# One pool group's u as a block product, in a hybrid attention and pooling layer

## The chip, the cores and the metric

The kernel runs on one core of one Trainium2 chip. The metric is the device time of one execution in microseconds. Several executions are timed, and the median counts; one more is recorded by the hardware profiler and gives the trace that is read below.

## The reference

One layer of a generator's backbone, for 1024 latent tokens and 256 context tokens of width 1024, in float32. A normalised and modulated input `h` goes through one wide projection, whose columns feed two branches. Branch A is a gated linear attention with four heads, run in both directions. Branch B is a pooling mixer in four groups of 256 columns, with windows of 2, 4, 8 and 16 tokens. Both are gated, projected, merged by sigmoid gates, projected again and normalised. What matters here is branch B and the projection that feeds it:

```python
p = h @ w_in
... uB, zB, gA, gB = jnp.split(p, idx, axis=-1)
# multiscale_pool: per group g with window w
parts.append((csg[:, hi + 1] - csg[:, lo]) / cnt - uf[..., sl])   # windowed mean minus u
y = einsum(d, w_pool) * pool_scale
yB = (y * jax.nn.silu(zB)) @ w_branch_b
```

## The kernel before

Matrices are kept transposed: `h^T` lies in eight row tiles of 128 rows, each in two token halves of 512 columns. To keep float32's precision every operand is split into a high and a low part (`split`, line 82: ScalarE writes the high part, VectorE the rest by a tensor_tensor of 512 columns), and a product is made of three matmuls, high x high, high x low and low x high. All matmuls are recorded on line 77.

There are two forms of a product. The plain one (`proj_t`, line 273) makes 128 output rows for 512 tokens by 8 x 3 matmuls into one PSUM bank, which ScalarE then empties. `pool_u` (line 643) and `pool_gate` (line 624) call it four times for a group, so 96 matmuls; their weights come by `wslot` (line 245), one load of 512 KB and two splits for 128 columns. The block form (`block_product`, line 797) makes 256 output rows for all 1024 tokens by seven products of blocks in place of eight (Winograd's form), each of 4 x 3 matmuls, so 84. The seven are, in order, L11 R11, S2 T2, S3 T3, S1 T1, L12 R21, L22 T4 and S4 R22. L and S are pieces of the weights: `block_weights` (line 762) loads two raw tiles, makes four sums or differences and splits all seven; this is called at high priority. R and T are operands of `h^T`: three of them are tiles of `h^T` itself, and T2, T3, T1, T4 are made once by `operands_h` (line 741) for each of four pairs of row tiles, with four additions, four subtractions and four splits on VectorE, in temporary tiles (tags `A` and `sw`, for the fourth pair `wh` and `wl`). The results are put in `h_ops` and serve all later block products. `take` (line 811) empties the banks: ScalarE copies product 1 into the output, VectorE adds the others. The banks are taken in the cycle sc, pj, sc, pj, pj (line 794), with two banks of tag sc and three of pj, so product 6 uses the bank of product 1.

Each pool group needs `u` (its columns of the projection), the gate `zb`, the difference `d` of the windowed mean and u (`pool_diff`, line 651: for each of two row tiles, passes over 1024 columns on VectorE, then a split of each token half) and the mix (`pool_mix`, line 688: 24 matmuls, a multiplication with the gate and the operands of the next product, which are written to DRAM). The groups are taken in the order 1, 0, 2, 3 (line 850). The tile of `u` has the tag `t8` with one slot: the next `u` can be written only when `d` has read the one before; GpSimd then fills the edges of the new tile (lines 639 and 640).

A framework orders the work. The program gives it the instructions with their tiles; when it is built, each engine's queue is laid out by priority (program order, with the weights of block products ahead) and by when operands and tile slots come free, and every wait is set by it. Tags with few slots matter here: `wr` (raw weights) 2, `wh` and `wl` (split weights) 4 each, `A` and `sw` 2 each, `t8` 1. Before the stretch around the change the last attention head uses most of them. The part that the change touches (lines 881 to 889):

```python
u[0] = pool_u(order[0])
zb[0] = pool_gate(order[0])
d[0] = [pool_diff(order[0], u[0][:, m, :]) for m in range(2)]
u[1] = pool_u(order[1])
for _ in range(4):
    add_h_ops()
pool_mix(order[0], d[0], zb[0])
d[1] = [pool_diff(order[1], u[1][:, m, :]) for m in range(2)]
u[2] = pool_u_blocks(order[2])
```

In the rows below the tile names are the tags: `t` is the tile of u, `z` a temporary of `pool_diff`, `qk` the gate, `s` the split difference, `ppj` and `psc` PSUM banks.

Of the kernel before, what the change touches and what calls it, by code (L numbers as in the profile page):

```python
# [34 lines left out]

# slots of the one SBUF pool, by tag; PSUM banks, by tag
BUFS = dict(h=32, wr=2, wh=4, wl=4, z=2, t8=1, lr=5, s2=8, sw=2, v=8, qk=8, bx=1, A=2, kt=2, S=6, S0=4, on=1,
# [5 lines left out]
def hybrid_kernel(ctx: ExitStack, tc: tile.TileContext, x, ctx_in, rows, w_mod, b_gate_row,  # L43
# [38 lines left out]
    def split(hi, lo, src):  # L82
        """src = hi + lo, exactly, both float32r"""
        act(hi, src)
        tt(lo, src, hi.bitcast(F32), ALU.subtract)
# [3 lines left out]

    # ---- constants and small vectors as columns  # L90
    cst = const("cst", [P, N_CONST])
    load(cst, consts)
    ident = cst[:, C_ID:C_ID + P]
    ones = cst[:, C_ONE:C_ONE + P]
# [15 lines left out]

    # ---- token tiles: load, root mean square, normalise
    pow_in = const("pow_in", [P, 10])
# [21 lines left out]

    # ---- low-rank gate inputs, stacked parts on partitions
    def low_rank_weights():
# [16 lines left out]

    # ---- modulation: shift and scale as columns [d, (latent, context)]
    sA = const("sA", [P, KT, 2])
# [7 lines left out]
    def modulate(kt, t0, n, c, ptag):  # L163
        """psum of one row tile of xn^T and the scale and shift that make it h^T"""
        pt = PT(ptag)
        for i in range(n // P):
            nc.tensor.transpose(pt[:, i * P:(i + 1) * P],
                                xs[t0 + i][kt // 4][:, (kt % 4) * P:(kt % 4 + 1) * P], ident)
        return pt[:, :n], sA[:, kt, c:c + 1], shA[:, kt, c:c + 1]
# [31 lines left out]
    for b in range(4):  # L201
        s_, half_ = b % 2, b // 2
        c0 = s_ * D + half_ * HALF
# [3 lines left out]
        for kt in range(KT):  # L207
# [8 lines left out]
            hi, lo = T("wh", [P, HALF], F32R), T("wl", [P, HALF], F32R)  # L216
# [24 lines left out]

    # ---- weight stream: slots of 1024 columns, split into exact float32r parts
    ahead = [False]

    def wslot(src, shape, col_scale=None):
        """rows [p, k, n] of a weight; per k: (hi, lo)"""
        _, nk, n = shape
        per = HALF // n
        parts = []
        with tc.high_priority() if ahead[0] else nullcontext():  # L250
            raw = T("wr", shape)
            load(raw, src)
            if col_scale is not None:
                tt(raw, raw, col_scale.rearrange("p (k n) -> p k n", k=1).to_broadcast(shape), ALU.mult)
            for k0 in range(0, nk, per):
                kn = min(per, nk - k0)
                hi, lo = T("wh", [P, kn, n], F32R), T("wl", [P, kn, n], F32R)
                split(hi, lo, raw[:, k0:k0 + kn, :])
                parts += [(hi[:, i, :], lo[:, i, :]) for i in range(kn)]
        return parts  # L260
# [4 lines left out]
    def wquad(w, c0, col_scale=None):  # L265
        """256 columns, all rows"""
        parts = []
        for kh in range(2):
            src = w[kh * HALF:(kh + 1) * HALF, c0:c0 + 256]
            parts += wslot(src.rearrange("(k p) n -> p k n", p=P), [P, 4, 256], col_scale)  # L270
        return parts

    def proj_t(w, rhs_hi, rhs_lo, n):
        """psum[128 columns, n tokens] = W^T h"""
        pt = PT("pj")
        nk = len(w)
        for k in range(nk):
            whi, wlo = w[k]
            mm(pt[:, :n], whi, rhs_hi[k], k == 0, False)
            mm(pt[:, :n], whi, rhs_lo[k], False, False)  # L280
            mm(pt[:, :n], wlo, rhs_hi[k], False, k == nk - 1)
        return pt

    def proj_n(w, lhs_hi, lhs_lo, tok):
        """psum[128 tokens, 256 columns] = h W"""
        pt = PT("pj")
        for k in range(KT):
            whi, wlo = w[k]
            mm(pt[:, :256], lhs_hi[k][:, tok], whi, k == 0, False)
            mm(pt[:, :256], lhs_hi[k][:, tok], wlo, False, False)  # L290
            mm(pt[:, :256], lhs_lo[k][:, tok], whi, False, k == KT - 1)
        return pt
# [25 lines left out]

    # ---- context: final states of both directions
    S0 = [None] * NH  # L320
# [28 lines left out]
    def transpose_k(src, tag):  # L349
        """four of [dk, 128] -> [token, chunk, dk]"""  # L350
        pt = PT("tr")
        for i in range(CPH):
            nc.tensor.transpose(pt[:, i * P:(i + 1) * P], src[i], ident)  # L353
        kT = T(tag, [P, CPH, P])
        act(kT, chunks(pt))
        return kT
# [32 lines left out]

    # ---- latent heads  # L390
    def rope_apply(pt, hf, scale):
# [37 lines left out]

    # Queries and keys lie with their two decays side by side: slot 1 is what a left block gives to the  # L430
    # scores with its right neighbour (backward decay of queries, forward of keys), slot 0 is for right blocks.
    # Decays of tokens and blocks: array 0 has the backward one of the even and the forward one of the odd,
    # array 1 the others.
    DEC_OFF = {2: 0, 4: 256, 8: 384, 16: 448, 32: 480, 64: 496, 128: 504}
# [8 lines left out]
    def level(t, hl):  # L443
        """slot 1 of the even blocks of hl tokens and slot 0 of the odd ones: [pair, block, token]"""
        t = t.rearrange("p n d -> p (n d)").rearrange("p (g x) -> p g x", x=4 * hl)[:, :, 1:4 * hl - 1]
        return t.rearrange("p g (s r) -> p g s r", s=2)[:, :, :, 0:2 * hl - 1:2]

    def gates(h):
        """per half: decays of the tokens, and of the blocks of 2, 4, .. 128 tokens"""
        both = T("bx", [P, 2, 2, HALF])  # L450
        e, one = [both[:, hf] for hf in range(2)], [None, None]
        for hf in (1, 0):
            one[hf] = [T("s2", [P, HALF]) for _ in range(2)]
            for d in range(2):
                pt = PT(('o', 'tr', 'sc', 'sc')[2 * hf + d])
                bcol = gate_in(pt, h, d, hf + 1, HALF)
                for t in range(2):
                    a = 0 if d != t else 1
# [30 lines left out]
    def double_q(hl, t, dec):  # L489
        """from blocks of hl tokens to blocks of 2 hl"""  # L490
        t = level(t, hl)
        dec = dec.rearrange("p (g s n) -> p g s n", s=2, n=1)[:, :, ::-1, :]
        tt(t, t, dec.to_broadcast([P, HALF // (2 * hl), 2, hl]), ALU.mult)

    def double_k(hl, cur, rest, dec):
        """the same; cur meets its sibling in the scores of a level"""
        shape = [P, HALF // (4 * hl), 2, hl]
# [6 lines left out]
    def head_scores(h, st, decays):  # L504
        """per half: scores within chunks; queries and keys with the decay up to the ends of their chunk:
        qf, qb, kf, kb by chunk; and the decays of the chunks, forward and backward"""
        one, e = decays
# [78 lines left out]

    # ---- context states and latent heads
    msk_f = T("bx", [P, len(LEVELS), P])
# [33 lines left out]

    # ---- pooling branch
    def pool_gate(g):
# [26 lines left out]
    def pool_diff(g, u):  # L651
        """split tiles of (windowed mean - u)^T for one row tile"""
        w = WINDOWS[g]
# [44 lines left out]

    # ---- products of 2 x 2 blocks by seven block products (Winograd's form):
    #      row blocks m of W^T, inner blocks j (odd and even row tiles), token halves hf  # L700
    half_tile = {}

    def slot2(tag, dt=F32R):
        """two tiles of 512 columns"""
        if tag in ("t8", "bx"):
# [17 lines left out]
    def block_operands(o, val):  # L723
        """splits the operands of a row tile pair from the values of R11, R12, R22, R21 (overwritten)"""
        def put(n, v):
# [15 lines left out]
    def operands_h(g, tags, temps):  # L741
        """block operands of h^T, row tiles 2g and 2g + 1"""
        k0, k1 = 2 * g, 2 * g + 1
# [53 lines left out]
    def block_product(w, c0, ops, outs, post, by_rows=False, pre=None):  # L797
        """outs[m][hf] = (W^T X) of two column tiles from c0; post(m, hf) when one is done"""
        with tc.high_priority():
# [46 lines left out]

    # ---- pool groups; block operands of h^T meanwhile
    h_tags = {"T2": ["v"] * 4, "T3": ["lr", "lr", "S0", "S0"], "T1": ["S", "S", "S", "A"], "T4": ["bx", "bx", "kt", "sw"]}
# [34 lines left out]
    zb[0] = pool_gate(order[0])  # L883
    d[0] = [pool_diff(order[0], u[0][:, m, :]) for m in range(2)]
    u[1] = pool_u(order[1])
    for _ in range(4):
        add_h_ops()
    pool_mix(order[0], d[0], zb[0])
    d[1] = [pool_diff(order[1], u[1][:, m, :]) for m in range(2)]
# [12 lines left out]

    # ---- gates of the merge
    def release_order(tags):
# [37 lines left out]
    for i in range(2):  # L942
        for mp in range(4):
            if (i, mp) != (0, 0):
                gate_pair(i, mp)
            if (i, mp) == (1, 1):
                gb_ops.append(gb_operands(0))
    # ---- pool branch output
    gb_ops += [gb_operands(g) for g in range(1, 4)]
# [16 lines left out]

    # ---- attention branch output, merged
    freed = release_order(b_tags)
# [34 lines left out]

    # ---- output projection, residual and final norm
    mH = [[None] * KT for _ in range(2)]
# [107 lines left out]
```

## Time and profile before

| | |
|---|---|
| median of three runs | 1150.31 us |
| lowest and highest run | 1150.07 and 1152.89 us |
| span of the profiled execution | 1152.8 us |
| TensorE (PE) busy | 1119.6 us, 97% |
| VectorE (DVE) busy | 812.2 us, 70% |
| ScalarE (ACT) busy | 493.4 us, 43% |
| mean granted clock of TensorE | 0.995 |

Of the profiled execution's own time only the span is known; it lies 0.1 us under the slowest of the three runs and 2.5 us over their median. The profile has a page with busy times, the span in 40 slices, queues, the chain of work that ended last and the costliest groups; and views of stretches of it, of which a timeline lists the instructions of an engine with their start, their length and, in brackets, how long the engine stood idle before and what released it. Matmuls overlap, so their listed lengths add up to more than the time they take; their pace is read from many in a row.

### The profile page before, as it was taken

The page shows a single profiled execution, that of the slowest core. Times are in us where ns is not written, and L with a number is a line of the kernel's source. Part 1 is how long each engine was busy: PE and PEld are TensorE (multiplying, and loading weights), DVE is VectorE, ACT ScalarE, POOL GpSimd, SP SyncE. Part 2 cuts the span into 40 slices and gives each one's busy share as a digit, 9 for nine tenths or more (in the row PEclk, how much of TensorE's full clock was granted, in tenths as well). Part 3 has the DMA queues.
Part 4 walks back from the last instruction along what each step waited for, and adds up shares of the span by engine and source line. Part 5 has one row for each costly group of instructions (what it writes and reads, how often), then busy time and mean ns, then how long its engine had stood idle before and what let it go on. Part 6 is the DMA issues. An engine that isn't in the chain of part 4 may idle for free.

```text
span 1152.8 us, 16292 instructions
## 1 busy us (share of the span) xinstructions
PE 1119.6 (97%) x5993; PEld 926.7 (80%) x5993; DVE 812.2 (70%) x1533; ACT 493.4 (43%) x962; POOL 24.2 (2%) x50
## 2 busy tenths in 40 slices
PE   6799999999999999999999999999999999999997
PEld 1268998798798798788888888888887886878997
DVE  4677458488588587698988867665768776757454
ACT  6697552462452552543333433343446324113233
POOL 0100000000000000100000000000000000000001
PEclk9899999999999999999999999999999999999999
DMA  8812150120220310103251463524448468982113
GB/s 292 291 37 74 42 151 28 56 73 20 65 65 20 85 44 20 55 28 119 82 161 50 128 201 119 167 84 129 151 137 269 161 197 287 298 302 94 38 38 146
DMA packets 119660, 138.40 MB, mean 120 GB/s; under 512 B 8803, under 2 KB 80669, under 8 KB 119454
## 3 DMA queue, kind: packets, MB, share of 16 engines
q1 hardware_dynamic: 119582, 137.38, 37.6%
q8 instruction: 47, 0.77, 0.3%
q14 instruction: 31, 0.25, 0.1%
HBM read 100.65 MB, written 32.51 MB: 116 GB/s over the span
## 4 chain that ended last, share of the span: by engine, by line
PE 86%; DMA 6%; ACT 2%; DVE 2%; issue 2%; SPq 1%; POOL 1%; POOLq 0%; ACTq 0%; DVEq 0%
PE ppj L77 59%; PE psc L77 19%; PE pst L77 3%; PE po L77 2%; DMA h<-w_mod 1%; DMA qk<-ga 1%; PE ptr L77 1%; DMA qk<-x 1%; DMA qk<-gb_T 1%; DMA wr<-w_in 1%; PE ptr L353 1%; ACT sw L63 1%; SPq L80 1%; DMA wr<-w_b 0%; DMA S<-ctx 0%
## 5 line engine op out<-in xcount | busy, mean ns | idle before, releaser
L77 PE MATMUL ppj<-h,wh 128*128 128x512 f32 x794 | 257.9, 401 | 1.0 <-ACT h L63 1.0
L63 ACT ACTIVATE wh<-wr 128x512 fp32r<-128x512 f32 (+1 forms) x183 | 113.7, 627 | 189.9 <-PE ppj L77 108.0
L77 PEld LDWEIGHTS ppj<-h,wh 128*128 128x128 f32 x794 | 146.8, 188 | 35.1 <-issue 2.9
L66 DVE TENSOR_TENSOR wl<-wr,wh 128x512 fp32r<-128x512 f32 (+1 forms) x183 | 124.8, 686 | 61.2 <-ACT wh L63 56.2
L77 PE MATMUL ppj<-wh,h 128*128 128x256 f32 x800 | 157.7, 283 | 0.0
L77 PE MATMUL ppj<-h,wl 128*128 128x512 f32 x397 | 157.2, 396 | 0.0
L77 PEld LDWEIGHTS ppj<-wh,h 128*128 128x128 f32 x800 | 129.9, 190 | 0.5 <-ACT qk L63 0.4
L77 PE MATMUL ppj<-wl,h 128*128 128x256 f32 x400 | 113.2, 283 | 0.0
L77 PEld LDWEIGHTS ppj<-h,wl 128*128 128x128 f32 x397 | 74.6, 188 | 15.1
L77 PEld LDWEIGHTS ppj<-wl,h 128*128 128x128 f32 x400 | 76.0, 190 | 0.2
L77 PEld LDWEIGHTS psc<-z,s 128*128 128x128 f32 x384 | 48.1, 188 | 9.8 <-issue 7.6
L487 DVE COPY_PREDICATED A<-msk,psc 128x512 f32<-128x512 uint8 x56 | 41.2, 735 | 19.8 <-PE psc L77 19.7
L77 PE MATMUL psc<-z,s 128*128 128x128 f32 x384 | 53.5, 280 | 0.0
L63 ACT ACTIVATE s<-s 128x512 f32<-128x512 f32 x60 | 36.9, 629 | 36.7 <-DVE s L66 31.6
L66 DVE TENSOR_TENSOR s<-s,ppj 128x512 f32<-128x512 f32 x60 | 40.7, 683 | 17.0 <-PE ppj L77 17.0
L63 ACT ACTIVATE s<-qk 128x256 f32<-128x256 f32 x56 | 23.1, 420 | 59.8 <-DVE qk L66 59.8
L74 DVE SCALAR_TENSOR_TENSOR S<-S,dec,pst 128x256 f32<-128x256 f32 x56 | 26.8, 478 | 26.3 <-PE pst L77 26.0
L77 PE MATMUL ppj<-S,wh 128*128 128x512 f32 (+1 forms) x132 | 41.2, 371 | 0.0
L77 PE MATMUL psc<-h,wh 128*128 128x512 f32 x126 | 39.1, 392 | 0.0
L66 DVE TENSOR_TENSOR s<-s,psc 128x512 f32<-128x512 f32 x43 | 29.2, 683 | 11.9 <-PE psc L77 10.2
L66 DVE TENSOR_TENSOR s<-s,bx 128x256 f32<-128x256 f32 (+1 forms) x64 | 30.5, 487 | 7.5 <-ACT bx L63 7.5
L66 DVE TENSOR_TENSOR on<-wr,wr 128x512 f32<-128x512 f32 x21 | 14.5, 691 | 30.0 <-DMA wr<-w_in 24.2
(518 smaller groups left out, 2390.3 us busy)
## 6 DMA issues: line engine op xcount, KB each, us to landing
wr<-w_in SPq DMA_DIRECT2D x65, 512.0 KB, 3.9
h<-w_mod SPq DMA_DIRECT2D x32, 256.0 KB, 5.4
qk<-sg SPq DMA_DIRECT2D x32, 256.0 KB, 5.3
sg<-s SPq DMA_DIRECT2D x28, 256.0 KB, 2.1
sw<-qk SPq DMA_DIRECT2D x64, 64.0 KB, 2.0
gb_T<-qk SPq DMA_DIRECT2D x16, 256.0 KB, 3.6
qk<-o SPq DMA_DIRECT2D x16, 256.0 KB, 4.7
ga<-s SPq DMA_DIRECT2D x16, 256.0 KB, 2.2
```

The source lines that it names most:

```text
L63: return nc.scalar.activation(out, in_, func, **kw)
L66: return nc.vector.tensor_tensor(out=out, in0=a, in1=b, op=op)
L74: return nc.vector.scalar_tensor_tensor(out=out, in0=a, scalar=s, in1=b, op0=op0, op1=op1)
L77: return nc.tensor.matmul(out, lhsT=lhsT, rhs=rhs, start=start, stop=stop)
L80: return nc.sync.dma_start(out=out, in_=in_)
L353: nc.tensor.transpose(pt[:, i * P:(i + 1) * P], src[i], ident)
L487: nc.vector.copy_predicated(A, msk[:, li:li + 1, :].to_broadcast([P, CPH, P]), chunks(pl))
```

## The change

Group 0, the second in the order, gets its u by the block form. Its operands must be there first, so the four calls of `add_h_ops` move ahead of it, and `d[0]` moves behind it in the program. The rest of the diff takes comments out.

```diff
 u[0] = pool_u(order[0])
 zb[0] = pool_gate(order[0])
-d[0] = [pool_diff(order[0], u[0][:, m, :]) for m in range(2)]
-u[1] = pool_u(order[1])
 for _ in range(4):
     add_h_ops()
+u[1] = pool_u_blocks(order[1])
+d[0] = [pool_diff(order[0], u[0][:, m, :]) for m in range(2)]
 pool_mix(order[0], d[0], zb[0])
 d[1] = [pool_diff(order[1], u[1][:, m, :]) for m in range(2)]
 u[2] = pool_u_blocks(order[2])
```

## Rows read from the trace of the kernel before

**Rows 1.** The page: busy time of each engine, and the granted clock in slices.
```profile
PE 1119.6 (97%) x5993; PEld 926.7 (80%) x5993; DVE 812.2 (70%) x1533; ACT 493.4 (43%) x962; POOL 24.2 (2%) x50
...
PEclk9899999999999999999999999999999999999999
```

**Rows 2.** Timeline of ScalarE, evictions of PSUM banks: start us, length us, instruction.
```profile
480.90 0.59 ACT L63 ACTIVATE t<-ppj 128x512 f32<-128x512 f32 x1
...
501.73 0.58 ACT L63 ACTIVATE qk<-ppj 128x512 f32<-128x512 f32 x1
...
523.12 0.60 ACT L63 ACTIVATE t<-ppj 128x512 f32<-128x512 f32 x1 [3.50 <-PE ppj L77]
...
537.86 0.58 ACT L63 ACTIVATE t<-psc 128x512 f32<-128x512 f32 x1
```

**Rows 3.** The chain that ended last, from 477 us: start us, length us, what.
```profile
477.02 51.50 PE ppj L77 x227
528.52 2.72 PE psc L77 x12
```

**Rows 4.** Busy us of each engine by stretch; then granted clock, DMA share, GB/s.
```profile
440.00:478.00 38.00, 36.90 (x198) 30.60 (x197) 25.88 (x51) 12.53 (x35) 2.07 (x3) 1.00 0.12 35
478.00:501.00 23.00, 23.00 (x103) 19.02 (x102) 22.84 (x39) 13.18 (x23) 1.15 (x3) 1.00 0.15 46
501.00:523.00 22.00, 22.00 (x99) 18.22 (x98) 19.24 (x31) 8.68 (x15) 0.00 (x0) 1.00 0.15 37
```

**Rows 5.** Timeline of VectorE from 479 to 521 us; idle time before in brackets.
```profile
479.13 0.68 DVE L66 TENSOR_TENSOR A<-A,A 128x512 f32<-128x512 f32 x1
479.73 1.22 DVE L74 SCALAR_TENSOR_TENSOR z<-z,t 128x1024 f32<-128x1024 f32 x1
...
485.21 1.24 DVE L66 TENSOR_TENSOR z<-z 128x1036 f32<-128x1036 f32 x1
486.36 0.69 DVE L66 TENSOR_TENSOR sw<-sw,sw 128x512 f32<-128x512 f32 x1
486.96 0.23 DVE L66 TENSOR_TENSOR z<-z,cst 128x2 f32<-128x2 f32 x2
...
496.91 0.69 DVE L66 TENSOR_TENSOR sw<-sw,A 128x512 f32<-128x512 f32 x1
...
499.93 0.69 DVE L66 TENSOR_TENSOR lr<-A,lr 128x512 fp32r<-128x512 f32 x1
...
512.01 0.69 DVE L66 TENSOR_TENSOR wh<-h,h 128x512 f32<-128x512 f32 x1 [1.39 <-PE ppj L77]
...
520.48 0.68 DVE L66 TENSOR_TENSOR sw<-wl,sw 128x512 fp32r<-128x512 f32 x1
```

**Rows 6.** Timeline of GpSimd, the fill of the tile of u.
```profile
537.40 0.11 POOL L639 MEMSET t<- 128x16 f32 x1 [48.18 <-DVE z L74]
```

**Rows 7.** The page, DMA issues: tiles, queue, count, KB each, us to landing.
```profile
wr<-w_in SPq DMA_DIRECT2D x65, 512.0 KB, 3.9
```

**Rows 8.** Timeline of SyncE's queue, loads of weights.
```profile
481.76 0.37 SPq L80 DMA_DIRECT2D wr<-w_in  x1
...
503.05 17.94 SPq L80 DMA_DIRECT2D wr<-w_in  x2
```

**Rows 9.** Busy us by stretch, with the granted clock third from the end.
```profile
54.00:55.00 1.00, 0.00 (x0) 0.00 (x0) 0.24 (x2) 0.69 (x2) 0.00 (x0) 1.00 0.00 0
55.00:56.00 1.00, 0.86 (x2) 0.47 (x2) 0.84 (x2) 0.97 (x3) 0.00 (x0) 0.56 0.00 0
56.00:57.00 1.00, 1.00 (x5) 0.79 (x5) 1.00 (x2) 0.64 (x2) 0.00 (x0) 0.50 0.00 0
57.00:58.00 1.00, 1.00 (x3) 0.54 (x2) 0.26 (x1) 1.00 (x3) 0.00 (x0) 0.50 0.00 0
58.00:59.00 1.00, 0.76 (x2) 0.32 (x2) 0.96 (x2) 1.00 (x3) 0.00 (x0) 0.73 0.00 0
...
960.00:965.00 5.00, 3.44 (x13) 1.97 (x12) 3.90 (x8) 2.42 (x4) 0.00 (x0) 1.00 1.04 380
```

## What was predicted, before the result was known

> **What bounds the kernel now.** I read the page first. TensorE (PE) is busy 97% of the span at full clock, VectorE (DVE) 70% [rows 1], so a change can only win by giving PE less to do, and can lose by making PE wait. Then the chain of waits around the edit: from 477 us on it is nothing but matmuls, 227 of them in 51.50 us, then block product after block product, 12 matmuls in 2.72 us [rows 3]. One 128x512 matmul therefore costs 0.227 us here. Third, who keeps up with whom: in 478 to 501 PE is busy 23.00 of 23.00 us and DVE 22.84; in 501 to 523 it is 22.00 and 19.24 [rows 4]. Two engines are full at once. PE sets the time, and DVE has next to no room in just the stretch where the edit lies. The reader should keep that in mind: the 70% of the page is a mean, here it is 99%.
>
> ScalarE's reads of the finished PSUM banks date the stage [rows 2]: u of the first group (u0) ends at 480.9, its gate (gate0) at 501.7, u of the second (u1) at 523.1. With 96 matmuls for a plain product, 96 x 0.227 = 21.8 us, u1's matmuls run from 501.2 to 523.0, and mix0 (24 matmuls, 5.45 us) follows.
>
> **What the change does to PE.** Plain u1 has 2 x 2 x 8 x 3 = 96 matmuls; the block form has 7 x 4 x 3 = 84 of the same shape. 12 x 0.227 = 2.72 us less PE work, on the path, if nothing makes PE wait.
>
> **What it does to DVE.** One 512-column tensor_tensor takes 0.604 us of DVE (five from 496.91 to 499.93) [rows 5]. Removed: four splits of plain weights, 4 x 0.604 = 2.4 us. Added: 4 subtractions and 7 splits for the block weights, 7 additions that combine the products, 18 x 0.604 = 10.9 us. Net +8.5 us, on an engine that is full. The 1.4 us that DVE waited for a weight slot at 512.01 [rows 5] goes, since the fourth operand set then uses slots that gate0 has left; that is credited by counting no wait there.
>
> **What is moved.** Before, u1's matmuls covered the making of the operands of h^T: 48 tensor_tensors (12 for each of four pairs of row tiles), the last starting at 520.48 [rows 5], two microseconds before u1 ended. After, u1 itself needs them, and the cover is gone: PE has nothing else, as mix0 waits for d0 and every later product for the operands. They cannot start earlier, since their slots are still the last attention head's; from 440 to 478 DVE is idle 12 of 38 us for such reasons [rows 4].
>
> I lay DVE's work from 479.13, the first subtraction of the first set [rows 5]; 4 of the 48 are done by then.
> - Product 1 (L11, R11) needs no new operand, product 2 needs T2 of all four pairs, and T2's split is the second last of a set, so 43 tensor_tensors come first: 26.0 us. One split for gate0 stands among them: 0.6. Weight pieces, which have priority: 3 subtractions and 5 splits, 4.8. T2 is whole at 479.1 + 31.4 = 510.5. PE starts u1 at 501.2, does 12 + 9 matmuls and is out of work at 506.0; it waits about 4.6 us. If the pieces not yet due (3 x 0.604) come later, T2 is whole at 508.7 and it waits 2.7.
> - From there 3 + 36 matmuls, 8.85 us, lead to the end of product 5: 519.5 (517.6 in the early case).
> - Product 6 needs the bank of product 1, and that is emptied into u1's tile, for which there is one slot, held by u0 until d0 has read it. Before, this wait is seen too: GpSimd's fill of the slot waits 48 us for DVE [rows 6]. So all of 44 tensor_tensors (26.6), gate0's split (0.6), nine weight operations (5.4) and d0 up to its last read come first. Of d0 there remain, from 479.73 on, the last wide pass of its first row tile and all three of the second, 4 x 1.15 (from 485.21 to 486.36), a short pair, 0.1, and the first tile's two splits, 1.2 [rows 5]: 5.9 us. Sum 38.5, so 517.6, and ScalarE's copy starts 0.5 after the release and takes 0.6, as at 537.40 and 537.86 [rows 2, 6]: 518.7. Whether d0 or the operands go first does not matter here, since both are due before product 6.
> - Product 6 thus starts at 519.5 (at least 518.7; 521.2 with the clock, below) instead of 501.2 + 5 x 2.72 = 514.8.
>
> **The clock.** When PE stood idle at 54 to 55 us, the granted clock then read 0.56, 0.50, 0.50 and 0.73 in the next four microseconds: 0.44 + 0.50 + 0.50 + 0.27 = 1.7 us of PE lost at 1.2 instead of 2.4 GHz. In 960 to 965, with 1.56 us idle in pieces, it stayed at 1.00 [rows 9]. A wait of 4.6 us in one piece is nearer to the first. I take 1.7 us in full, 0 as the other end. The Trainium skill (TensorE: Matmul & The Clock Gate, Part 1: The HAM clock gate) says the array's clock is gated to half by default and that activity releases it; the rows agree. By that rule the sum is as given; without it it would be 1.7 us lower.
>
> So product 6 starts at 519.5 + 1.7 = 521.2, u1 ends at 521.2 + 2 x 2.72 = 526.6 instead of 523.0: +3.6 us. DVE is not packed quite as tightly as I laid it: it idles 0.16 us in 478 to 501 and, without the slot wait, 1.4 in 501 to 523 [rows 4, 5]; I take +0.5 (0 to 1.5).
>
> **What is late next.** d1 needs u1 whole, and u2 waits for u1's slot as u1 does for u0's. Before, from u1's end to u2's first eviction it takes 537.86 - 523.0 = 14.9 us [rows 2]. After, d1's first row tile (2.4), d0's last splits (1.2) and the last combining addition (0.6) fall in there as well: 19.1. PE needs the bank after mix0 and five products, 5.45 + 13.6 = 19.05 less 0.6 for the copy, 18.4. That is 0 to 0.8 us of a second wait; I take 0.4, and 2.5 as the far end. Further on nothing changes but DVE's backlog.
>
> **Edits with no cost.** The weights of u1 are two loads of 512 KB either way; the second is issued at 481.76 [rows 8], lands 3.9 us later [rows 7] and is not due before 501. On SyncE's queue they keep their place; the load of mix0's weights follows them as before. u2's two loads, before from 503.05 to 521 [rows 8], start when u1's pieces are cut, the first some 10 us later, the second about as before, and are due at 532. Without that cover each would cost its 4 us. On GpSimd nothing is queued behind the fill of u1's slot. On ScalarE the first eviction of u1 waits for d0; behind it are the first halves of the next splits, and ScalarE has room.
>
> **Sum.** 3.6 + 0.5 + 0.4 = +4.5 us, ends 518.7 + 5.45 - 523.0 = +1.2 and 3.6 + 1.5 + 2.5 = +7.6. The profiled span is 1152.8 us, the slowest of the three runs 1152.89 and their median 1150.31; the sum is a difference of a few microseconds inside one stage and I put it on the median: 1154.8 (1151.5 to 1157.9).
>
> **Rivals.**
> - DVE keeps up (not slower). If T2 is whole by 506.0 and u0 read by 513.6, only the saving is left: 1150.31 - 2.72 = 1147.6. That needs 5 us less DVE work ahead of product 6 than I count, by operands or pieces made in the idle 12 us before 478. For it: that idle time, and that u1's first weights lie ready early. Against: the second half of the weights is issued at 481.76 [rows 8], and the operands' slots. It decides at those 5 us. 0.20.
> - Weight pieces of the product after u2, which have priority (11 x 0.604 = 6.6 us), go ahead of d1 and hold u2 up: 19.1 + 6.6 - 18.4 = 7.3 us at most, about 4.5 in the middle: 1159. For it: DVE is full up to 567 as well. Against: their slots come free only while u2 runs. 0.09.
> - The instruction order is set when the program is built; with the program changed, the later order may shift either way by a few microseconds, or put mix0 into the gap (up to 5.45 us of cover). 0.05.
>
> **How the numbers follow.** The forecast has 0.66. A measurement of this kernel can tell 0.3%, 3.45 us, from no change. Of the 0.66, spread over +1.2 to +7.6, 0.46 lies above that bound and 0.20 below. Slower: 0.46 + 0.09 + 0.01 = 0.56. Same: 0.20 + 0.18 of the first rival + 0.01 = 0.39. Faster: 0.05, as PE's saving alone, 2.72 us, does not reach the bound. The range takes in the first rival at its low end, 1147.3, and the forecast's far end with part of the second rival, 1158.6; about 0.1 is left out.
>
> **What would show it.** In the profile after: 84 matmuls for u1; a gap on PE of 3 to 5 us near 506, ended by the fourth T2 split; the granted clock at 0.5 for about 3 us behind it; a second, short wait of product 6 that traces back to d0; DVE without idle time from 478 to 530. No gap, or one under 2.7 us in sum, and I am wrong.

## The result, and the profile of the changed kernel

The changed kernel takes 1163.47 us (median of four runs, 1163.09 to 1164.35), the kernel before beside it 1150.22 (four runs). The ratio is 1.0108 with an interval of 1.0088 to 1.0127, so the change costs 12.4 us (10.1 to 14.6). The direction was forecast, but only about a third of the size.

The page of after, busy time of each engine, to be read beside [rows 1]:

```profile
PE 1119.2 (96%) x5981; PEld 926.2 (80%) x5981; DVE 820.5 (71%) x1547; ACT 494.3 (43%) x962; POOL 24.2 (2%) x50
```

Twelve matmuls fewer, 14 VectorE instructions and 8.3 us of VectorE more: the change does what it says. PE's busy time fell by 0.4 us only, though 12 x 0.227 = 2.72 us were saved, in part because some matmuls ran at half the clock (below). The rest is waiting. Here is every idle time of PE that the timeline lists from 490 to 565 us; the number in brackets is the idle time ahead of the instruction and its releaser:

```profile
501.13 0.73 PE L77 MATMUL psc<-lr,wh 128*128 128x512 f32 x2 [1.08 <-ACT wh L63]
503.56 0.50 PE L77 MATMUL psc<-h,wl 128*128 128x512 f32 x1 [1.70 <-DVE wl L66]
524.18 1.22 PE L77 MATMUL psc<-bx,wh 128*128 128x512 f32 x2 [5.89 <-ACT t L63]
552.72 0.72 PE L77 MATMUL psc<-bx,wh 128*128 128x512 f32 x2 [1.73 <-ACT t L63]
```

Before, PE has none there: matmuls follow on one another [rows 3]. The first two lie early in u1 and wait for pieces of its weights (tag `wh` is the high part of a piece, `wl` the low). The first is for the high part of S3, since PE does two matmuls of product 3 early (`lr` is a T3); the second is product 1, which waits for the low part of L11. The third and longest is product 6 (`bx` is T4), which waits for ScalarE's copy of product 1 into the tile of u. The fourth is the same wait in u2. By stretch, columns as in [rows 4]:

```profile
493.00:501.00 8.00, 7.05 (x32) 5.49 (x30) 8.00 (x14) 4.09 (x8) 0.00 (x0) 1.00 0.00 0
501.00:509.00 8.00, 6.17 (x19) 4.62 (x20) 6.56 (x12) 3.39 (x7) 0.00 (x0) 0.79 0.00 0
509.00:517.00 8.00, 8.00 (x37) 6.50 (x35) 7.74 (x14) 4.16 (x7) 0.00 (x0) 1.00 0.20 55
517.00:525.00 8.00, 2.11 (x8) 1.47 (x7) 7.50 (x12) 2.73 (x5) 0.15 (x2) 0.77 0.36 112
525.00:533.00 8.00, 8.00 (x30) 6.36 (x29) 6.95 (x12) 1.95 (x4) 0.00 (x0) 0.80 0.00 0
```

VectorE is full from 493 to 501 and then busy 82 to 97%, 94% of the stretch in which PE falls to 2.11 of 8. The clock falls twice, in 501 to 509 and from 521 on. First and last microsecond of each fall that PE worked in (between them it is 0.50):

```profile
504.00:505.00 1.00, 1.00 (x5) 0.75 (x4) 1.00 (x3) 0.25 (x1) 0.00 (x0) 0.63 0.00 0
...
507.00:508.00 1.00, 1.00 (x4) 0.83 (x3) 0.04 (x1) 0.70 (x2) 0.00 (x0) 0.67 0.00 0
...
524.00:525.00 1.00, 0.82 (x2) 0.72 (x3) 1.00 (x3) 1.00 (x3) 0.00 (x0) 0.50 0.00 0
...
528.00:529.00 1.00, 1.00 (x5) 0.78 (x5) 0.90 (x2) 0.09 (x1) 0.00 (x0) 0.93 0.00 0
```

A second trace of the kernel before (c0_before, below) lies on the same times as after until the edit, while in the first one everything in this stage is 1.7 us later. So after is compared with the second. The last product of attention, ahead of the edit, and the first matmul of mix0, behind u1, in PE's timeline of after:

```profile
473.77 0.70 PE L77 MATMUL po<-v,A 128*128 128x256 f32 x2 [0.81 <-ACT on L63]
...
531.64 0.61 PE L77 MATMUL ppj<-s,wh 128*128 128x512 f32 x2
```

The same two in c0_before:

```profile
473.83 0.70 PE L77 MATMUL po<-v,A 128*128 128x256 f32 x2 [0.83 <-ACT on L63]
...
521.25 0.61 PE L77 MATMUL ppj<-s,wh 128*128 128x512 f32 x2
```

u1 thus takes 10.4 us more. Its first matmul is at 499.43, so it takes 32.2 us: 84 x 0.227 = 19.1 of matmuls, 1.08 + 1.70 + 5.89 = 8.7 of waiting, 0.37 + 0.50 + 0.50 + 0.33 = 1.7 lost to the first fall of the clock and 0.82 x 0.50 + 3 x 0.50 + 0.07 = 2.0 to the second; 0.7 is not placed. With u2's wait the stage loses 10.4 + 1.7 = 12.1. Some of it comes back later. Before, PE stands 2.59 us near 887 (c0_before), waiting for a split of weights, and the clock falls behind that wait: it reads 0.81, 0.50, 0.50, 0.50 and 0.98 from 888 to 893, which is 1.7 us lost. After, the wait is still there, but shorter, and the clock stays at 1.00. PE's timeline of c0_before, then of after:

```profile
887.35 0.74 PE L77 MATMUL ppj<-h,qk 128*128 128x512 f32 x2 [2.59 <-ACT qk L63]
...
892.95 0.50 PE L77 MATMUL po<-t,wl 128*128 128x512 f32 x1 [0.41 <-DVE wl L66]
...
897.44 0.73 PE L77 MATMUL ppj<-h,qk 128*128 128x512 f32 x2 [1.01 <-ACT qk L63]
```

So 2.59 - 0.41 - 1.01 = 1.2 us of waiting and 1.7 of clock come back. That leaves 12.1 - 2.9 = 9.2, and the spans differ by 9.7 (1161.5 against 1151.8). The measured 12.4 lies above the 9.7 by 2.7, the lower end of its interval, 10.1, by 0.4. Single runs of the kernel before lie 3 us apart, so this difference can't be traced further.

Who ended u1's long wait? The chain that ended last, of after, from 516 us:

```profile
516.23 0.62 DVE wl L66
...
516.87 4.04 DMA wr<-w_in
...
520.93 0.69 DVE on L66
521.62 0.14 DVE z L66 x2
521.76 0.60 DVE wr L66
522.37 1.15 DVE z L74
...
523.53 0.61 ACT t L63
...
524.18 4.86 PE psc L77 x12
```

It runs backwards from product 6 over ScalarE's copy to d0's last read of u0 (`z` of line 74, the release of u's one slot), and from there into VectorE's queue. In that queue stand, ahead of the read, a split and two sums of u2's weights (the sums are `on` and `wr`). The sums wait for the second of u2's two loads, which could start only when mix0's weights had been split out of their raw tile (`wl` at 516.23). So the load of the next product lies on the path of this one, though VectorE had other work during most of it and stood idle for 0.47 us.

### The profile page after: what moved, and what is told of

Read it like the earlier page. It is cut to its first block, busy times and chain, and to the rows that moved or that the text cites. A ratio compares the mean times of both kernels' runs of the same rounds, so it can differ in the third digit from the quotient of the medians.

```text
span 1161.5 us, 16299 instructions
## 1 busy us (share of the span) xinstructions
PE 1119.2 (96%) x5981; PEld 926.2 (80%) x5981; DVE 820.5 (71%) x1547; ACT 494.3 (43%) x962; POOL 24.2 (2%) x50
## 4 chain that ended last, share of the span: by engine, by line
PE 86%; DMA 5%; DVE 4%; ACT 2%; issue 1%; POOL 1%; SPq 1%; POOLq 0%; DVEq 0%; ACTq 0%
PE ppj L77 58%; PE psc L77 20%; PE pst L77 3%; PE po L77 2%; DMA h<-w_mod 1%; PE ptr L77 1%; DMA wr<-w_in 1%; DMA qk<-x 1%; PE ptr L353 1%; DMA qk<-gb_T 1%; DVE wl L66 1%; ACT sw L63 1%; POOL r L581 1%; SPq L80 1%; DMA S<-ctx 0%
## 5 line engine op out<-in xcount | busy, mean ns | idle before, releaser
L77 PE MATMUL ppj<-h,wh 128*128 128x512 f32 x742 | 242.4, 402 | 1.6 <-ACT h L63 1.0
L77 PEld LDWEIGHTS ppj<-h,wh 128*128 128x128 f32 x742 | 137.0, 188 | 34.2 <-issue 2.9
L77 PE MATMUL ppj<-h,wl 128*128 128x512 f32 x371 | 147.2, 397 | 0.0
L77 PEld LDWEIGHTS ppj<-h,wl 128*128 128x128 f32 x371 | 69.7, 188 | 14.0
L77 PE MATMUL psc<-h,wh 128*128 128x512 f32 x138 | 44.0, 400 | 0.0
```

The costliest lines, as they stand in the source:

```text
L77: return nc.tensor.matmul(out, lhsT=lhsT, rhs=rhs, start=start, stop=stop)
```

## The experiments

Besides c0_before, three questions were put: is it VectorE's amount of work, or the slot, or the order (e1 to e3); does work taken off VectorE come back as time (e4 to e6, e8, e10); what does VectorE work cost by itself (e9, e11, e12). Edits are against the changed kernel unless said otherwise. For each kernel the sum of PE's idle times in 490 to 565 us stands beside its time. Each ratio is to runs of the kernel before that were taken beside it; rows whose intervals overlap are not told apart.

| kernel | PE waits, us | ratio to before (95%) |
|---|---|---|
| the change | 10.40 | 1.0108 (1.0088 to 1.0127) |
| e1_d0_first | 10.92 | 1.0112 (1.0090 to 1.0135) |
| e2_move_only | 1.28 | 1.0015 (1.0001 to 1.0029) |
| e3_aside | 11.35 | 1.0146 (1.0121 to 1.0170) |
| e4_adds_pool | 14.92 | 1.0124 (1.0109 to 1.0139) |
| e5_d0_qk | 9.18 | 1.0089 (1.0072 to 1.0106) |
| e6_d0_qk_pool | 16.03 | 1.0146 (1.0131 to 1.0161) |
| e8_no_adds | 3.26 | 1.0009 (0.9996 to 1.0022) |
| e9_before_more | 6.05 | 1.0078 (1.0052 to 1.0103) |
| e10_d0_qk_no_adds | 2.43 | 0.9994 (0.9984 to 1.0005) |
| e11_before_half | 2.33 | 1.0022 (1.0009 to 1.0036) |
| e12_half_adds | 7.04 | 1.0062 (1.0036 to 1.0089) |

**c0_before**, the kernel before once more, for a second trace.

> The kernel before, unchanged, for a second trace. If the trace on record is typical, its span is again about 1152.8 us; if that execution was a slow one, the span is 1148 to 1150, and the stretches in which the two traces differ say where. Both theories below expect u1 to be followed by mix0 without a gap on PE.

Span 1151.8; no idle time of PE from 490 to 565. It gave the comparison above.

**e1_d0_first**: d0 ahead of the operands, as in the kernel before.

```diff
 zb[0] = pool_gate(order[0])
+d[0] = [pool_diff(order[0], u[0][:, m, :]) for m in range(2)]
 for _ in range(4):
     add_h_ops()
 u[1] = pool_u_blocks(order[1])
-d[0] = [pool_diff(order[0], u[0][:, m, :]) for m in range(2)]
```

> The changed kernel with d0 back ahead of the operands in the program; u1 stays a block product. Theory V (VectorE is full: what counts is the sum of its work due before u1's product 6, whatever its order): d0 goes earlier and the operands later, product 6 starts at most 3 us earlier, 1159 to 1163 us. Rival S (the one slot of u: d0 stands last in VectorE's queue, behind weight pieces of u2, and holds u1's first eviction): the 5.9 us wait of product 6 and the clock fall behind it (2.0 us) go, 1154 to 1157 us.

The time is that of the change. The wait for the slot is gone, and a longer one stands in product 1, behind a short one for L11's high part:

```profile
500.65 0.73 PE L77 MATMUL psc<-h,wh 128*128 128x512 f32 x2 [1.27 <-ACT wh L63]
...
509.82 0.79 PE L77 MATMUL psc<-h,wl 128*128 128x512 f32 x1 [7.92 <-DVE wl L66]
```

The 7.92 us (PE's timeline of e1) are for L11's low part; on VectorE it stands directly behind temporaries of the fourth operand set, which have the same tag `wl`:

```profile
508.48 0.69 DVE L66 TENSOR_TENSOR wl<-h,h 128x512 f32<-128x512 f32 x1
509.08 1.28 DVE L66 TENSOR_TENSOR wl<-wr,wh 128x512 fp32r<-128x512 f32 x2
```

It looks as if the slots of a tag go out in program order: a piece of the weights, of high priority, waits for the temporaries that the program names before it. That is inferred from this order; e5, below, fits it. Mix0 begins at 531.13, against 531.64. The order of d0 and operands decides where PE waits; in sum it waits about as long (10.92 against 10.40).

**e2_move_only**: the lines as in the change, but u1 plain.

```diff
-u[1] = pool_u_blocks(order[1])
+u[1] = pool_u(order[1])
```

> The changed order (operands, u1, then d0), but u1 stays the plain product. Theory V: 8.5 us of VectorE work are not there and u1 needs no operand, so PE waits little, 1149 to 1152 us. Rival S: the slot of u is still held by d0 behind the operands; the fourth of u1's four evictions' banks is missing and PE waits 3 to 6 us near the end of u1, 1153 to 1157 us.

0.15%, 1.7 us: one wait of 1.28 us and mix0 1.8 later than in c0_before. Moving the lines without the block product costs next to nothing; u1's plain product, which needs no operand, still covers them.

**e3_aside**: product 1 is emptied into tiles of another tag, which need no release by d0; four copies on ScalarE bring u into its tile.

```diff
+def pool_u_aside(g):
+    outs = [[T("h", [P, HALF]) for _ in range(2)] for _ in range(2)]
+    block_product(w_in, O_UB + g * 256, h_ops, outs, lambda m, hf: None)
+    u = pool_pad()
+    for m in range(2):
+        for hf in range(2):
+            act(u[:, m, PAD + hf * HALF:PAD + (hf + 1) * HALF], outs[m][hf])
-u[1] = pool_u_blocks(order[1])
+u[1] = pool_u_aside(order[1])
```

> The changed kernel, with u1's block product written to four tiles of freed rows of h^T and copied from there into the tile of u by ScalarE, so that product 6 no longer waits for d0. Rival S: the wait of 5.9 us and the clock fall behind it go, 1154 to 1157 us. Theory V: product 6 starts on time, but VectorE is as late as before, and what it owes (d0's splits for mix0, the combining additions, u2's pieces) is waited for instead, 1158 to 1162 us.

u1's long wait is gone and mix0 begins at 521.72, ten microseconds earlier. It helps nothing: the same waits follow in mix0 and u2, in PE's timeline of e3:

```profile
533.16 1.65 PE L77 MATMUL ppj<-s,wh 128*128 128x512 f32 x3 [3.16 <-ACT s L63]
...
553.36 1.22 PE L77 MATMUL psc<-bx,wh 128*128 128x512 f32 x2 [5.07 <-ACT t L63]
```

So the slot was the place where VectorE's delay met PE, not its cause. With it away PE meets the delay at the next things that VectorE makes, d0's splits (`s`) and d1.

**e4_adds_pool**: the 16 additions of `operands_h`, 9.7 us, on GpSimd, which is idle.

```diff
-    tt(v, f(hH[hf][kt]), f(hL[hf][kt]), ALU.add)
+    nc.gpsimd.tensor_tensor(out=v, in0=f(hH[hf][kt]), in1=f(hL[hf][kt]), op=ALU.add)
```

> The changed kernel with the 16 additions that rebuild h^T in the operand sets (hi + lo) on GpSimd in place of VectorE; nothing else differs. Theory V (VectorE's sum of work is the bound): 16 x 0.604 = 9.7 us less on VectorE ahead of product 6, GpSimd has the time; product 6 starts 6 to 9 us earlier, 1152 to 1157 us. Rival W (the weight pieces L11 and on wait for slots that the fourth operand set holds, in program order, so the order of the slots is the bound): the fourth set's temporaries are still handed out first and GpSimd takes longer for each addition; no gain, 1162 to 1168 us.

No faster than the change, with a wait of 13.36 us for L11's high part in u1. VectorE was not relieved. GpSimd's timeline of e4, an addition while VectorE stands idle and one beside its work:

```profile
473.82 1.27 POOL L747 TENSOR_TENSOR sw<-h,h 128x512 f32<-128x512 f32 x1 [0.43 <-DMA o<-sw]
...
488.40 1.74 POOL L747 TENSOR_TENSOR A<-h,h 128x512 f32<-128x512 f32 x1
```

VectorE's timeline of e4, beside an addition and while GpSimd pauses:

```profile
490.62 1.78 DVE L66 TENSOR_TENSOR A<-A,A 128x512 f32<-128x512 f32 x1
...
496.33 0.68 DVE L66 TENSOR_TENSOR sw<-sw,A 128x512 f32<-128x512 f32 x1
```

A tensor_tensor takes VectorE 0.68 us alone and 1.78 beside one of GpSimd, which takes 1.74 then and 1.27 alone. VectorE's starts move from 0.60 to 1.70 us apart, so an addition moved away that meets VectorE's work costs VectorE 1.1 us where it saved 0.6.

The Trainium skill (SBUF — State Buffer, "SBUF: two separate sides") says that the two engines share a pair of ports as an exclusive lock, held for a whole instruction, also by a VectorE operation with two SBUF inputs. The trace agrees as far as it goes: 1.70 us for one of each is near, though under, 0.60 + 1.27 = 1.87.

**e5_d0_qk** and **e6_d0_qk_pool**: e1 with the fourth set's temporaries under a tag with eight slots, so that the weights don't wait for them; e6 has e4's additions as well.

```diff
-("A", "A", "sw", "sw") if k < 3 else ("wh", "wh", "wl", "wl")))
+("A", "A", "sw", "sw") if k < 3 else ("qk",) * 4))
```

> The changed kernel with d0 ahead of the operands, as in e1, and the fourth operand set's four temporaries in the gate's free tiles (tag qk) in place of the weights' slots (wh, wl). In e1 PE stood 7.9 us for the low part of L11, which got its slot only after the fourth set had taken its own. Rival W: product 1 starts at once, the 7.9 us wait and the half clock behind it shrink to a wait of 2 to 4 us for the fourth T2, 1153 to 1157 us. Theory V: VectorE has the same sum to do, PE only waits later, for T2 of the fourth set in product 2, 1158 to 1163 us.

> Both together: d0 first, the temporaries of the fourth set in qk, and the 16 additions on GpSimd. If VectorE's sum and the slots are all that is behind the loss, PE runs through u1 with at most 2 us of waiting, and the 12 saved matmuls show: 1148 to 1153 us. If GpSimd's additions are slow enough to hold the sets up (over 1.5 us each), 1156 to 1164 us.

e5: the waits in u1 shrink to 0.37, 0.64, 1.80 and 0.16, and mix0 begins at 525.99. Then u2 waits for d1, and most of it is lost again (PE's timeline of e5):

```profile
551.53 1.22 PE L77 MATMUL psc<-bx,wh 128*128 128x512 f32 x2 [6.21 <-ACT t L63]
```

e6 is the slowest with e3, and slower than either of its expectations; its longest wait is 10.86 us, in u1. It is clearly slower than e5, from which it differs by the additions on GpSimd alone, so the loss of e4 is not one of slots only.

**e8_no_adds** and **e10_d0_qk_no_adds**: the change, and e5, without the 16 additions. The subtractions read the high parts of `h^T` only, so the low parts are missing from T1 to T4.

```diff
-for v, (hf, kt) in zip(val, ((0, k0), (1, k0), (1, k1), (0, k1))):
-    tt(v, f(hH[hf][kt]), f(hL[hf][kt]), ALU.add)
...
+tt(t1, h12, h11, ALU.subtract)
+tt(t3, h22, h12, ALU.subtract)
+tt(t2, h22, t1, ALU.subtract)
+tt(t4, h21, t2, ALU.subtract)
...
```

> The changed kernel without the 16 additions (hi + lo) that begin the operand sets: the subtractions read the high parts of h^T instead, so the low parts are left out of T1 to T4. That takes 16 x 0.604 = 9.7 us off VectorE ahead of product 6 and adds nothing to GpSimd. Theory V (VectorE's work due before u1's products is the bound): product 6 starts 7 to 9 us earlier and one fall of the clock goes, 4 to 10 us faster than the changed kernel, ratio to the kernel before 1.001 to 1.006. Rival W (slots handed out in program order): L11 still waits for the fourth set's slots, at most 3 us faster, 1.008 to 1.011.

> d0 first and the fourth set's temporaries in qk, as in e5, and without the 16 additions (the low parts are left out of T1 to T4). If VectorE's room is all that the block form of u1 lacks, PE runs through u1 and u2 with under 2 us of waiting and the 12 saved matmuls show: ratio 0.997 to 1.000. If it lies in something else that the block form brings (more evictions, banks, u2's wait for d1), 1.003 to 1.008.

With 9.7 us less on VectorE the whole loss is gone, within the intervals: 1.0009 and 0.9994. In e8 PE doesn't wait in u1, and mix0 begins at 518.31; the last product of attention lies 0.4 earlier than in c0_before, so u1 is 2.5 us shorter than the plain one. That is the saving of 2.72, seen by itself. But u2 takes it back (PE's timeline of e8):

```profile
541.14 1.22 PE L77 MATMUL psc<-bx,wh 128*128 128x512 f32 x2 [3.26 <-ACT t L63]
```

The stretch after that wait, by the columns of [rows 4]:

```profile
541.00:549.00 8.00, 7.86 (x22) 6.25 (x23) 5.45 (x9) 0.71 (x2) 0.00 (x0) 0.62 0.01 2
```

PE is busy nearly throughout, but at a clock of 0.62. Even with a part of the computation left out, the block form of u1 wins nothing that can be measured.

**e9_before_more**: the kernel before, with 14 further tensor_tensors in `operands_h` (maxima of a tile with itself): 8.5 us on VectorE, as much as the change adds, but with u1 plain and all cover kept.

```diff
     tt(v, f(hH[hf][kt]), f(hL[hf][kt]), ALU.add)
+for v in val[:4 if g < 2 else 3]:
+    tt(v, v, v, ALU.max)
```

> The kernel before with 14 more tensor_tensors of 512 columns on VectorE (8.5 us, the maximum of an operand's value with itself), put into the four operand sets; u1 stays plain and covers them. Theory V1 (VectorE's sum over the whole stage is the bound): it idles 4.6 us from 478 to 567, so 4 us or more are left over and PE waits for them, ratio 1.003 to 1.008. Theory V2 (only what is due before a near deadline counts, and the cover by u1's plain matmuls was what kept it off): the last operand is 10 us ahead of its use, so nothing waits, 0.999 to 1.002.

0.78%, 9.0 us (6.0 to 11.9). u1 isn't touched (mix0 begins at 521.34), and u2 pays (PE's timeline of e9):

```profile
547.02 1.22 PE L77 MATMUL psc<-bx,wh 128*128 128x512 f32 x2 [5.06 <-ACT t L63]
```

**e11_before_half** has seven of the 14 maxima (`val[:2 if g < 3 else 1]`), and **e12_half_adds** is the change with the additions of the first two operand sets left out, as in e8.

> The kernel before, u1 plain, with 7 further tensor_tensors of 512 columns on VectorE in the making of the operands (maxima of a tile with itself, which change no value): 7 x 0.604 = 4.2 us, half of the dose that cost 0.78%. Two theories of the price. L (every microsecond that VectorE gets on top is paid, as it has no room left): half the dose costs half, +4.5 us, 0.39%. T (a threshold: VectorE's idle time in 478 to 600, some 9 us, takes up a small dose, and the price jumps when PE's wait is long enough to bring the clock down): +1 us or less, under 0.1%, with the clock at 1.00 in 541 to 549.

> The changed kernel with 8 of its 16 additions of parts left out, those of the first two sets (their low parts are missing from T1 to T4): VectorE has 4.8 us less to do before u1, half of the step that took the time from +1.1% back to +0.1%. L: halfway between the two, about +7 us, 0.6%. T: near one of the two ends, so within 2 us of +1 (PE's waits in u1 short, clock at 1.00) or of +13 (first eviction of u1 still waits 5 us or more for d0, clock at 0.5 after it).

e11: 0.22%, 2.5 us (1.0 to 4.2), between the two theories; one wait of PE:

```profile
545.57 0.73 PE L77 MATMUL ppj<-h,wh 128*128 128x512 f32 x2 [2.33 <-DVE t L66]
```

The clock did not fall (third from the end, in the stretch of that wait):

```profile
541.00:549.00 8.00, 5.67 (x25) 4.36 (x24) 7.97 (x14) 2.98 (x7) 0.00 (x0) 1.00 0.01 4
```

e12: 0.62%, 7.1 us (4.2 to 10.3), as L expected. On the kernel before, 4.2 us of VectorE cost 2.5 and 8.5 cost 9.0, so the second half of the dose costs 6.5 (both intervals are wide; half of 9.0 lies just outside that of e11). On the change, leaving out 4.8 us gains 12.4 - 7.1 = 5.3 and leaving out 9.7 gains 11.4. So the first microseconds seem to be partly taken up; after that each costs one or more. One reason is the clock: in e9 it is 0.50 behind the wait of 5.06 us, from 547 to 551, and in e11 it stays at 1.00.

## Why the prediction fell short

**Right.** PE's saving is there (2.5 of 2.72 in e8). VectorE's net load was forecast at +8.5 us and measured at +8.3. The cause is that load on a full engine, and e9 and e8 show it from both sides. "Whether d0 or the operands go first does not matter" holds for the time (e1). The reason given, that both are due before product 6, is not what e1 shows: there it is product 1 that waits. The working also saw that product 6 depends on u's one slot. And PE came to the end of product 5 at 524.18 - 5.89 = 518.3, which in the first trace's times is 520.0, against 519.5 to 521.2. That agreement is luck: the wait for T2 that was laid there did not come, and others took its place (below).

The sum has one small slip: 510.5 + 8.85 is 519.4 and not 519.5.

**The step that failed: VectorE's work ahead of the slot's release.** By the prediction the slot was ready first (copy done at 518.7) and PE's own products came last (519.5), so product 6 had no long wait. It was the other way round. The prediction laid 38.5 us; from the same subtraction (`A<-A,A`, 477.44) to the end of d0's last read it took 523.5 - 477.4 = 46. Rows of VectorE's timeline of after, the first, and those that the sum didn't have:

```profile
477.44 0.68 DVE L66 TENSOR_TENSOR A<-A,A 128x512 f32<-128x512 f32 x1
...
484.75 0.69 DVE L66 TENSOR_TENSOR on<-wr,wr 128x512 f32<-128x512 f32 x1 [1.10 <-DMA wr<-w_in]
...
507.96 0.69 DVE L66 TENSOR_TENSOR wl<-on,wh 128x512 fp32r<-128x512 f32 x1 [1.44 <-ACT wh L63]
...
519.78 0.68 DVE L66 TENSOR_TENSOR h<-wr,h 128x512 fp32r<-128x512 f32 x1
520.93 0.69 DVE L66 TENSOR_TENSOR on<-wr,wr 128x512 f32<-128x512 f32 x1 [0.47 <-DMA wr<-w_in]
...
521.68 0.68 DVE L66 TENSOR_TENSOR wr<-wr 128x512 f32<-128x512 f32 x1
522.28 1.22 DVE L74 SCALAR_TENSOR_TENSOR z<-z,t 128x1024 f32<-128x1024 f32 x1
```

The 44 operand instructions, 26.6 us, are as laid. Of weight instructions there are 15 instead of nine: two more of u1, one of mix0, and three of u2, the last three in front of d0's final read. That is 6 x 0.604 = 3.6 us. Idle time, laid as none in the 38.5 (the sum added 0.5 for it, 1.5 at most), is 1.10 + 1.44 + 0.26 + 0.47 = 3.3, for weight loads and slots; with 0.6 of smaller gaps that makes the 7.5. ScalarE's copy ends at 523.53 + 0.60 = 524.13, which is 525.8 in the first trace's times, against 518.7. Product 6 is then held up by d0 and not by PE's own products, for 5.9 us.

**The rival that was half seen.** The pieces of a following product ahead of a difference were put on u2 and d1, with a chance of 0.09. It happened one group earlier, u2's pieces ahead of d0. With them came the load itself: "without that cover each would cost its 4 us" was written of PE, and counted at nothing. PE did not wait for it, but VectorE's queue did, by 1.10 us for the load of u1 and 0.47 for that of u2.

**The waits early in u1.** The forecast gap near 506, ended by the fourth T2, did not come; PE went on with matmuls of products 3 and 4 whose operands were whole, between those of product 2. In its place came 1.08 us for S3's high part, which ScalarE cuts only at 500.47, and 1.70 for L11's low part, which VectorE cuts at 502.82, behind two temporaries of the fourth set with the same tag (501.62). That the fourth set's slots were taken as free ("counting no wait there") is a second, smaller step that failed. e5, which takes those temporaries out of the tag, shrinks the waits in u1, though it doesn't bring the time back.

**The clock.** One fall of 1.7 us was counted; there were two, 1.7 + 2.0.

**What is late next.** u2's second wait was put at 0.4 with 2.5 as the far end; it is 1.73.

**What a better sum would have been.** The experiments fit a balance over the stage, not over the one product. VectorE is idle for 9 of the 122 us from 478 to 600 in c0_before, and little of this gets filled: with more work laid on it, it is busy 113.61 us there in e9, and 114.26 in e11. Here is c0_before:

```profile
478.00:600.00 122.00, 122.00 (x537) 100.50 (x536) 112.78 (x176) 52.16 (x89) 0.47 (x6) 1.00 0.30 93
```

So when 8.5 us are laid on it, PE waits for most of that, whichever deadline it meets first: u1's slot (the change), L11 (e1), mix0 and u2 (e3), mainly u2 (e5, e9). The prediction followed one deadline with care, asked of the next only whether d1 was late by a little, and let PE's own running time absorb the rest. By the balance, 8.5 us and two falls of the clock, less PE's 2.7, give 8.5 + 3.7 - 2.7 = 9.5, where the stage lost 12.1. The rest may be VectorE's own waiting for loads and slots, 3.3 us in u1; that is not shown. The balance is a rough one: the same work on VectorE cost 10.3 us in e5 (1.0089) and 16.8 in e3 (1.0146).

## What to carry to other kernels

Where two engines are full in the same stretch, a change that takes work from one and gives more to the other can lose about what it gives or more, wherever the first wait appears. Here freeing that wait (another slot, another order) only moved it, and the clock that fell with the waits was a part of the cost (3.7 of the stage's 12.1 us). Price such a trade by a run that adds the second engine's work alone to the kernel before. When laying an engine's queue by hand, count what belongs to the next product too, with the loads that it waits for, since a priority puts it ahead of older work.

## What the runs showed of the hardware that was not expected

GpSimd and VectorE slow each other on tensor_tensors in SBUF (0.68 to 1.78 us, and 1.27 to 1.74), so that an idle GpSimd was no help (e4, e6). The Trainium skill (Perfetto Trace Analysis, Optimizing Scalar/DVE Operations) warns that offloading between these two might not help; e4 and e6 agree.

The granted clock stayed at 1.00 after single waits of PE of 1.73 us (the change, u2), 2.33 (e11, near 545) and 2.98 (e11, near 890). It fell to 0.50 at 3.26 (e8) and 5.89 (the change), but also behind 2.12 (e9, near 895) and 2.59 (c0_before, near 887), and after 1.08 and 1.70 us with 0.7 us of work between them. So among single waits of 2 to 3 us their length alone did not decide in these runs.
